# Attention on one core: four pairs of heads turned by transfers, one more group of exponentials on VectorE, and a new order

## The chip, the core and the metric

The kernel runs on one core of one Trainium2 chip. The core's engines work side by side: TensorE (PE) multiplies matrices, VectorE (DVE), ScalarE (ACT) and GpSimd (POOL) work elementwise, and SyncE (SP) issues transfers (DMAs). The metric is the device time of one execution in microseconds. Before the change it was 114.85 us, the median of three runs (114.81 to 115.61).

## The reference

Softmax attention over 8 batches of 8 heads, 512 positions and 64 dimensions, in and out as 32-bit floats:

```python
scale = 1.0 / np.sqrt(q.shape[-1])
scores = np.einsum('bhqd,bhkd->bhqk', q, k) * scale
scores = scores - scores.max(axis=-1, keepdims=True)
attn = np.exp(scores)
attn = attn / attn.sum(axis=-1, keepdims=True)
return np.einsum('bhqk,bhkd->bhqd', attn, v)
```

The kernel subtracts no maximum. It multiplies by a fixed factor within the exponential, and gives `v` a column of ones, so that the sum of the weights comes out of the same matmul as the values; the division stands at the end.

## The kernel before, in words

**Pairs.** The 64 heads are taken as 32 pairs, numbered 0 to 31. For each pair `k`, `q` and `v` are loaded as 256 KB transfers (L487), all issued by SyncE. GpSimd casts them to 16 bits (`cast`): `k` and `q` into a tile `qkp` (L503), `v` into one of twelve tiles `vp` (L493). Seven raw tiles per tensor exist, so a load waits for the cast of the pair seven before it.

**Turning.** The scores need `q` and `k` with the head dimension on the partitions. TensorE transposes eight blocks of 128x128 of `qkp` into a tile of PSUM (`transposes`, L534), and VectorE copies it to `tqk` (`copy`, L547). Pair 0 has its own start (`first_pair`).

**Scores and exponentials.** A group is two blocks of 128 keys by 512 queries. `scores` (L574) writes one group into one of three PSUM tiles `st`. There are 129 groups, the last two of which are the two query halves of one. ScalarE takes the exponential of a group in one instruction (L578) and writes `pt`. Sixteen groups, listed in `ON_DVE`, go to VectorE instead: `raise_` (L598) turns scores into the bits of a 16-bit float, and five passes (L615, L624, L632, L634, L638) correct it. The result is two tiles, `pe` and `pd`, the sum of whose products is wanted, so each such block costs two value matmuls instead of one.

**Values.** `values` (L670) accumulates, for each head, four units of 128 queries by 64 columns and the column of sums. Seven units fill a PSUM tile `o`. VectorE takes the reciprocals (`reciprocal`, L644), multiplies (`normalise`, L649), and writes the units into a ring of 112 units in SBUF. `store` (L660) sends a head (four units, 128 KB) from the ring to memory. All but one of the 63 heads that pass through the ring are stored by SyncE; one, the first head of the last pair, goes out on ScalarE's queue. The very last head has its own path: `last_values` (L686) and `finish` (L699 to L706), which normalises it into `obl` and stores it by SyncE.

**What sets the order.** The class `Plan` plays all engines through with fixed costs in nanoseconds and writes down the order of steps. The kernel is emitted in this order, and on each engine the instructions run in the order in which they are emitted. The plan decides, for each engine, what comes next: SyncE has loads first (`step_sp`), stores when no load is possible or more than `URGENT` stores are outstanding; TensorE has scores first, then transposes, then values (`step_pe`); VectorE has copies, raises, reciprocals and products first, passes in between (`step_dve`). The constants `LATE_...`, `HURRY`, `SOON`, `PAIR`, `DUEK`, `DUEV`, `DUEL` and `PRE` shift these decisions and the times by which casts are due. A transfer that SyncE issues waits in its place for what it needs, and all later ones wait behind it. Eight completion semaphores are used in turn, so that a transfer also waits for the landing of the eighth before it.

In the profile, a line beginning with L is a line of the code below. SPq and ACTq mark issues of transfers by SyncE and by ScalarE.

Of the kernel before, what the change touches and what calls it, by code (L numbers as in the profile page):

```python
# [9 lines left out]
FP32 = mybir.dt.float32  # L10
# [7 lines left out]
class Plan:  # L18
# [15 lines left out]
    STEP = 5  # L34
    CALM, KEEN = 9000, 4
    FIRST_UNIT = 4
    ON_DVE = (5, 11, 15, 24, 36, 41, 49, 55, 60, 70, 76, 83, 94, 105, 109, 120)

    LATE_NORM, LATE_COPY, HURRY, SOON, BACKLOG = 2300, 700, 1000, 200, 700
    LATE_MUL, WAIT = 400, 200  # L40
    SLACK, AHEAD = 0, 2

    CAST, CAST_PORT, CAST_DONE, TO_POOL = 557, 475, 130, 150
    SCALE_PORT, PRODUCT_PORT, GAP, REACH = 265, 533, 20, 5
    FIRST_LAND, LOAD, STORE, LATENCY, ISSUE = 5200, 740, 370, 2300, 470
    QUEUED, URGENT = 3500, 16
    RAW, QK16, NV, NU = 7, 5, 12, 112
    PAIR, DUEK, DUEV, DUEL, PRE = 3300, 2800, 4000, 7000, 0

    def __init__(self, groups, pairs, first):  # L50
        self.groups, self.pairs = groups, pairs
        self.pe, self.act, self.dve = 7000, self.FIRST_EXP, 6300
        self.pool, self.port, self.dma = 4600, 4600, self.FIRST_LAND
        self.m, self.tiled = first, True
        self.read = []
        self.exps = {}
        for m in range(first):
            self.act += self.EXP + self.EXP_FIXED
            self.exps[m] = self.act + self.EXP_DONE
            self.read.append(self.exps[m])  # L60
        self.tq = {0: 5800}
        self.transposed = {0: 5800}
        self.next_t = 1
        self.part_t = 0
        self.banks = [5100, 5800]
        self.todo = [(g, h) for g in range(pairs) for h in range(2)]
        self.last = self.todo.pop()
        self.last_part = 0
        self.head = None
        self.units = self.FIRST_UNIT  # L70
        self.member = {b: m for m, grp in enumerate(groups) for b in grp}
        self.ready = []
        self.passes = []
        self.passed = {}
        self.raised = set()
        self.steps = []
        self.busy_dve = 0
        self.done_heads = 0

        late = {grp[0][0] for m, grp in enumerate(groups) if m in self.ON_DVE}  # L80
        due = []
        for g in range(pairs):
            scores = 5000 + self.PAIR * g
            if g:
                due += [(scores - self.DUEK, g, "k"), (scores - self.DUEK + 10, g, "q")]
            due.append((scores + self.DUEV + (self.DUEL if g in late else 0), g, "v"))
        self.due = sorted(due)
        self.uncast = list(self.due)
        self.casts = []
        self.landed, self.cast_done = {}, {}  # L90
        self.first_loads = [(g, n) for _, g, n in self.due if g < self.RAW]
        self.first_loads += [(self.RAW, "k"), (self.RAW, "q")]
        for x in self.first_loads:
            self.dma += self.LOAD
            self.landed[x] = self.dma
        self.loads, self.stores, self.stored = [], [], []
        self.sp = 1650 + 470 * len(self.first_loads)

    def note(self, t, *what):
# [51 lines left out]
                self.cast_done[(g, n)] = begin + self.CAST + self.CAST_DONE  # L151

    def step_sp(self, t):
        if self.sp > t or self.dma > t + self.QUEUED:
            return
        urgent = len(self.stores) > self.URGENT
        if self.loads and not urgent:
            g, n = self.loads[0]
            if self.cast_done.get((g - self.RAW, n), 1e9) <= t:
                self.loads.pop(0)  # L160
                self.note(t, "load", g, n)
                self.dma = max(self.dma, t + self.LATENCY - self.LOAD) + self.LOAD
                self.landed[(g, n)] = self.dma
                self.sp = t + self.ISSUE
                return
        if self.stores and self.stores[0] <= t:
            self.stores.pop(0)
            self.note(t, "store")
            self.dma = max(self.dma, t + self.LATENCY - self.STORE) + self.STORE
            self.stored.append(self.dma)  # L170
            self.sp = t + self.ISSUE
# [66 lines left out]
    def last_values(self, t):  # L238
        end = len(self.groups)
        if self.m < end or self.last_part == 4:  # L240
            return False
        part = self.last_part
        read = self.exps.get(end - (3, 3, 2, 1)[part], 1e9)
        if t < max(read, self.cast_done.get((self.last[0], "v"), 1e9)):
            return False
        self.note(t, "last", part)
        self.full(t, self.V_UNIT)
        if part == 3:
            self.ready.append((self.pe + self.TO_DVE, "finish", ()))
        self.last_part += 1  # L250
        return True

# [36 lines left out]
    def step_pe(self, t):  # L289
        if self.m == len(self.groups):  # L290
            self.values(t)
            return
        g = self.groups[self.m][0][0]
        backlog = self.act - t
        one, two = self.free() <= t, self.free(1) <= t
        if one and (two or backlog < self.HURRY or self.tiled):
            return self.scores(t)
        if not one and backlog < self.BACKLOG and self.free() < t + self.SOON:
            return
        if self.part_t:  # L300
            return self.transposes(t)
        if (
            self.next_t < self.pairs
            and self.next_t <= g + self.AHEAD
            and all(self.cast_done.get((self.next_t, n), 1e9) <= t for n in "kq")
            and self.bank(t) is not None
        ):
            return self.transposes(t)
        if not self.values(t) and one:
            self.scores(t)  # L310

    def step_dve(self, t):
# [14 lines left out]
        if now:  # L327
# [22 lines left out]
                for _ in range((what[0] + what[1]) // 4 - what[0] // 4):  # L350
                    self.stores.append(self.dve + 100)
            elif kind == "finish":
                self.dve = t + self.RECIPROCAL + self.PASS_DONE + self.NORM[0] + 4 * self.NORM_COLUMN
            elif kind == "copy":
                held, done = self.COPY if what[0] != 1 else self.COPY_1
                self.dve = t + held
                self.banks[what[1]] = self.tq[what[0]] = t + done + self.TO_PE
            else:
                self.dve = t + self.RAISE[0]
                self.read[what[0]] = t + self.RAISE[1] + self.TO_PE  # L360
                self.raised.add(what[0])
                self.passes += [(what[0], s) for s in range(len(self.PASSES))]
                self.passed[what[0], None] = self.dve + self.PASS_DONE
# [43 lines left out]
def kernel(  # L407
# [28 lines left out]
    cpool = ctx.enter_context(tc.tile_pool(name="const", bufs=1))  # L436
    lpool = ctx.enter_context(tc.tile_pool(name="load", bufs=7))
    qpool = ctx.enter_context(tc.tile_pool(name="qk16", bufs=5))
    tpool = ctx.enter_context(tc.tile_pool(name="tqk", bufs=4))
    ppool = ctx.enter_context(tc.tile_pool(name="pt", bufs=24))  # L440
    dpool = ctx.enter_context(tc.tile_pool(name="pd", bufs=4))
    wpool = ctx.enter_context(tc.tile_pool(name="work", bufs=Plan.BITS))
# [83 lines left out]
    def transposes(g, n, bank):  # L526
# [7 lines left out]
            reads[g] = nc.tensor.transpose(tps[g][:, n, i, :], qkp[g][:, n, i, :], ident)  # L534
        if g == 1 and n == 1:
            copy(g, n)

    def copy(g, n=0):
        if g == 1:
# [116 lines left out]

    def store():
        g, h, u0 = heads.pop(0)
        queue = nc.scalar if (g, h) == (LAST, 0) else nc.sync
        queue.dma_start(out=source(out, g)[:, h], in_=ring[:, u0 % NU : u0 % NU + NI, :])  # L660

    def values(g, h, y, u, bank):
# [13 lines left out]
            )  # L676

    def last_values(part):
        if part == 0:
            last["o"] = ps_st.tile([P, 2, S], FP32, tag="st", name="o_last")[  # L680
                :, 0, 0 : NI * (D + 1)
            ].rearrange("p (x d) -> p x d", x=NI)
        half, late = ((0, 0), (1, 0), (0, 1), (1, 1))[part]
        for c in (2 * late, 2 * late + 1):
            for x in (2 * half, 2 * half + 1):
                nc.tensor.matmul(  # L686
                    last["o"][:, x, :],
                    blocks[(LAST, c, 1)][0][:, x * P : (x + 1) * P],
                    vps[LAST % NV][:, 1, c, :],
                    start=(c == 0 and x == 0),  # L690
                    stop=(c == NI - 1),
                    skip_group_check=True,
                )

    def finish():
        o = last["o"]
        ob = opool.tile([P, NI, D], FP32, tag="obl", name="obl", bufs=1)
        rc = opool.tile([P, 7, 1], FP32, tag="rc", name="rc_last")
        nc.vector.reciprocal(out=rc[:, 0:NI], in_=o[:, :, D : D + 1])  # L699
        nc.vector.tensor_tensor(  # L700
            out=ob[:, :, :],
            in0=o[:, :, 0:D],
            in1=rc[:, 0:NI].broadcast_to([P, NI, D]),
            op=AluOp.mult,
        )
        nc.sync.dma_start(out=source(out, LAST)[:, 1], in_=ob[:, :, :])  # L706

    def first_loads():
        tk = load_tile(0, "k")
# [99 lines left out]
    with tc.manual_schedule():  # L809
# [6 lines left out]
        for n in range(NV):  # L816
# [5 lines left out]
            "values": values,  # L822
            "load": load,
            "store": store,
            "cast": cast_behind,
            "raise": raise_,
            "copy": lambda g, b: copy(g),
# [38 lines left out]
```

## Time and profile before

| What | Number |
|---|---|
| median of three runs | 114.85 us |
| the profiled execution | 114.75 us |
| its span, first to last instruction | 113.0 us |
| ScalarE busy | 105.6 us (93%) |
| TensorE busy | 103.8 us (92%) |
| VectorE busy | 101.4 us (90%) |
| GpSimd busy | 64.9 us (57%) |
| bytes moved by transfers | 33.84 MB, 300 GB/s on the mean |

The span is the time from the first instruction to the last; the execution's own time has some more around it. A busy time is the time in which an engine has an instruction running; SyncE has no such number, as issuing isn't counted as busy. Rows of groups give the line, engine and operation, the tiles (out<-in) and their shapes, the count, then busy time and mean length in ns, and the idle time before. Rows of a timeline give start and length in us.

### The profile page before, as it was taken

What the parts mean: (1) busy time and instruction counts of PE and PEld (TensorE: products, weight loads), DVE (VectorE), ACT (ScalarE), POOL (GpSimd) and SP (SyncE); (2) the same over time, 40 slices, a digit from 0 to 9 for tenths busy, and PEclk for the clock granted to TensorE, in tenths of its full rate; (3) what the DMA queues carried; (4) which work ended last, traced back from release to release, by engine and by line L of the source; (5) the groups of instructions that cost most, each with busy time, mean ns of one, the idle gap of its engine ahead of it and who ended that gap; (6) DMA issues with size and microseconds to landing.
All of it is one profiled execution on the core that took longest, in us unless ns stands there. A gap on an engine that the chain in (4) does not pass through costs nothing.

```text
span 113.0 us, 4341 instructions
## 1 busy us (share of the span) xinstructions
PE 103.8 (92%) x1687; PEld 68.9 (61%) x1687; DVE 101.4 (90%) x226; ACT 105.6 (93%) x118; POOL 64.9 (57%) x127
## 2 busy tenths in 40 slices
PE   7979989899999998899999999999999999999940
PEld 2634646567665575575677567677668665775730
DVE  1567999999989999999999999999999999999560
ACT  4699999999999999999999999999999999999930
POOL 2167896275478858668667987846866993000000
PEclk9999999999999999999999999999999999999995
DMA  3999999999999999999999989999993978828744
GB/s 98 273 335 354 349 348 347 346 348 348 348 349 343 345 332 350 348 358 312 340 358 331 292 244 338 339 345 331 369 363 102 298 264 267 275 93 266 249 131 156
DMA packets 35381, 33.84 MB, mean 300 GB/s; under 512 B 2592, under 2 KB 35360, under 8 KB 35360
## 3 DMA queue, kind: packets, MB, share of 16 engines
q1 hardware_dynamic: 34928, 33.17, 91.5%
q10 hardware_dynamic: 432, 0.39, 1.0%
q8 instruction: 13, 0.21, 0.9%
q14 instruction: 8, 0.07, 0.2%
HBM read 25.17 MB, written 8.39 MB: 297 GB/s over the span
## 4 chain that ended last, share of the span: by engine, by line
PE 45%; DVE 42%; ACT 7%; issue 2%
PE o L670 19%; PE st L574 15%; DVE pd L598 9%; DVE tqk L547 8%; DVE ring L649 7%; PE tp L534 7%; ACT pt L578 7%; DVE m L632 4%; DVE pd L638 3%; PE st_0a L717 3%; DVE pe L624 2%; DVE m L615 2%; DVE m L634 2%; DVE rc L644 2%; PE st L760 1%
## 5 line engine op out<-in xcount | busy, mean ns | idle before, releaser
L578 ACT ACTIVATE pt<-st 128x1024 f16<-128x1024 f32 (+1 forms) x110 | 100.4, 1096 | 0.0
L670 PEld LDWEIGHTS <-pt 128*128 128x128 f16 x880 | 38.9, 98 | 12.6 <-issue 10.8
L670 PE MATMUL o<-vp,pt 128*128 128x65 f16 x880 | 46.3, 194 | 0.2
L574 PE MATMUL st<-tqk 64*128 64x512 f16 (+1 forms) x250 | 42.4, 381 | 2.5 <-ACT pt L578 1.8
L503 POOL CAST qkp<-k 128x512 f16<-128x512 f32 x31 | 21.5, 693 | 11.6 <-DMA k<-in_k_dram 5.2
L493 POOL CAST vp<-v 128x512 f16<-128x512 f32 x32 | 21.7, 696 | 7.9 <-DVE rc L644 2.6
L503 POOL CAST qkp<-q 128x512 f16<-128x512 f32 x30 | 21.3, 710 | 6.7 <-DVE rc L644 3.3
L649 DVE TENSOR_TENSOR ring<-o,rc 128x448 f32<-128x448 f32 (+2 forms) x37 | 22.4, 607 | 0.6
L670 PE MATMUL o<-vp,pe 128*128 128x65 f16 x128 | 22.1, 195 | 0.0
L670 PE MATMUL o<-vp,pd 128*128 128x65 f16 x128 | 21.9, 193 | 0.0
L534 PE MATMUL tp<-ident,qkp 128*128 128x128 f16 x248 | 19.9, 220 | 1.0 <-DVE ring L649 0.7
L547 DVE COPY tqk<-tp 128x1024 f16<-128x1024 f16 x30 | 20.4, 680 | 0.2 <-PE tp L534 0.2
L598 DVE TENSOR_SCALAR pd<-st 128x1024 uint16<-128x1024 f32 x16 | 19.5, 1218 | 0.7 <-PE st L574 0.7
L534 PEld LDWEIGHTS <-qkp 128*128 128x128 f16 x248 | 14.3, 97 | 7.9 <-issue 4.0
L574 PEld LDWEIGHTS <-tqk 64*128 64x128 f16 x250 | 11.6, 93 | 11.7 <-issue 4.3
L670 PEld LDWEIGHTS <-pe 128*128 128x128 f16 x128 | 12.5, 98 | 3.8 <-issue 2.9
L670 PEld LDWEIGHTS <-pd 128*128 128x128 f16 x128 | 12.6, 98 | 0.0
L638 DVE TENSOR_TENSOR pd<-pd,m 128x1024 f16<-128x1024 f16 x16 | 10.9, 683 | 0.0
L632 DVE TENSOR_TENSOR m<-m 128x1024 f16<-128x1024 f16 x16 | 10.9, 683 | 0.0
L644 DVE RECIPROCAL rc<-o 128x7 f32<-128x7 f32 (+2 forms) x37 | 7.3, 198 | 1.9 <-PE o L670 1.9
L624 DVE TENSOR_SCALAR pe<-pd 128x1024 uint16<-128x1024 uint16 x16 | 6.8, 424 | 0.0
L615 DVE TENSOR_SCALAR m<-pd 128x1024 uint16<-128x1024 uint16 x16 | 6.6, 413 | 0.0
(50 smaller groups left out, 33.3 us busy)
## 6 DMA issues: line engine op xcount, KB each, us to landing
v<-in_v_dram SPq DMA_DIRECT2D x32, 256.0 KB, 5.8
k<-in_k_dram SPq DMA_DIRECT2D x31, 256.0 KB, 5.9
q<-in_q_dram SPq DMA_DIRECT2D x31, 256.0 KB, 5.8
out_dram<-ring SPq DMA_DIRECT2D x62, 128.0 KB, 3.7
k<-in_k_dram ACTq DMA_DIRECT2D x2, 128.0 KB, 2.8
q<-in_q_dram SPq DMA_DIRECT2D x2, 128.0 KB, 2.6
out_dram<-ring ACTq DMA_DIRECT2D x1, 128.0 KB, 1.9
out_dram<-obl SPq DMA_DIRECT2D x1, 128.0 KB, 2.0
```

Source lines behind the costliest of these rows:

```text
L493: return nc.gpsimd.tensor_copy(out=vps[g % NV][:, :, :, 0:D], in_=raw[g]["v"][:, :, :, :])
L503: return nc.gpsimd.tensor_copy(out=dst, in_=src[:, :, :, :])
L534: reads[g] = nc.tensor.transpose(tps[g][:, n, i, :], qkp[g][:, n, i, :], ident)
L547: nc.vector.tensor_copy(out=tqk[g][:, :, :], in_=tps.pop(g).rearrange("p n i c -> p n (i c)"))
L574: nc.tensor.matmul(st[:, x, cols], kc, qc[:, cols], start=True, stop=True)
L578: nc.scalar.activation(out=pt[:, :, cols], in_=st[:, :, cols], func=EXP, scale=scale, bias=SHIFT)
L598: nc.vector.tensor_scalar(out=r["pd"][:, :, :], in0=r["st"][:, :, :], scalar1=BITS, scalar2=BIAS, op0=AluOp.mult, op1=AluOp.add,)
L632: ins = nc.vector.tensor_tensor(out=m16, in0=m16, in1=m16, op=AluOp.mult)
L638: ins = nc.vector.tensor_tensor(out=u16, in0=u16, in1=m16, op=AluOp.mult)
L644: dve(nc.vector.reciprocal(out=rcs[u][:, 0:n], in_=o[:, x : x + n, D : D + 1]))
L649: nc.vector.tensor_tensor(out=ring[:, u % NU : u % NU + n, :], in0=o[:, x : x + n, 0:D], in1=rcs.pop(u)[:, 0:n].broadcast_to([P, n, D]), o ...
L670: nc.tensor.matmul(os[u // 7][:, u % 7, :], part[:, y * P : (y + 1) * P], vps[g % NV][:, h, c, :], start=(n == 0), stop=(n == len(parts) - 1),
```

## The change

The planner gets a new step, `turn`. Pairs 28 to 31 (`TURNED = 28`) are no longer transposed by TensorE and copied by VectorE. SyncE issues one transposing transfer for each, from `qkp` straight into `tqk`, of which there are now eight tiles instead of four. The casts of `k` and `q` of these pairs are made due earlier (`TURN_AHEAD`). `ON_DVE` lists 17 groups instead of 16, at other places. The last head is handled in two halves of the queries: two tiles for its values, two reciprocals and products, two stores of 64 KB by SyncE. The last two stores from the ring go out on ScalarE's queue. Other constants of the plan are changed, so that the whole order is made anew: the places of casts, loads, stores and passes differ all through the kernel.

On SyncE, the changed kernel issues 163 transfers in place of 159. Ahead of the first `turn` stand 123: all loads but one, and stores. Then follow: the turn of pair 28 (issue 124), the load of the last `v`, nine stores, the turns of pairs 29 and 30 (135 and 136), eight stores, the turn of pair 31 (145), sixteen stores, and the two halves of the last head (162 and 163).

```diff
--- before.py
+++ after.py
@@ -34,18 +34,20 @@
     STEP = 5
     CALM, KEEN = 9000, 4
     FIRST_UNIT = 4
-    ON_DVE = (5, 11, 15, 24, 36, 41, 49, 55, 60, 70, 76, 83, 94, 105, 109, 120)
-
-    LATE_NORM, LATE_COPY, HURRY, SOON, BACKLOG = 2300, 700, 1000, 200, 700
-    LATE_MUL, WAIT = 400, 200
+    ON_DVE = (5, 11, 17, 24, 30, 39, 45, 54, 59, 69, 75, 79, 88, 96, 104, 112, 120)
+
+    LATE_NORM, LATE_COPY, HURRY, SOON, BACKLOG = 1100, 1800, 700, 160, 700
+    LATE_MUL, WAIT = 1200, 200
     SLACK, AHEAD = 0, 2
 
     CAST, CAST_PORT, CAST_DONE, TO_POOL = 557, 475, 130, 150
-    SCALE_PORT, PRODUCT_PORT, GAP, REACH = 265, 533, 20, 5
+    SCALE_PORT, PRODUCT_PORT, GAP, REACH = 271, 537, 20, 5
     FIRST_LAND, LOAD, STORE, LATENCY, ISSUE = 5200, 740, 370, 2300, 470
     QUEUED, URGENT = 3500, 16
     RAW, QK16, NV, NU = 7, 5, 12, 112
-    PAIR, DUEK, DUEV, DUEL, PRE = 3300, 2800, 4000, 7000, 0
+    TURNED, TQ = 28, 8
+    TURN, TURN_LATENCY, TURN_ISSUE, TURN_AHEAD, TURN_MARGIN = 2500, 4300, 1450, 7500, 200
+    PAIR, DUEK, DUEV, DUEL, PRE = 3300, 3550, 5500, 1000, 1250
 
     def __init__(self, groups, pairs, first):
         self.groups, self.pairs = groups, pairs
@@ -82,7 +84,8 @@
         for g in range(pairs):
             scores = 5000 + self.PAIR * g
             if g:
-                due += [(scores - self.DUEK, g, "k"), (scores - self.DUEK + 10, g, "q")]
+                ahead = self.DUEK if g < self.TURNED else self.TURN_AHEAD
+                due += [(scores - ahead, g, "k"), (scores - ahead + 10, g, "q")]
             due.append((scores + self.DUEV + (self.DUEL if g in late else 0), g, "v"))
         self.due = sorted(due)
         self.uncast = list(self.due)
@@ -94,6 +97,7 @@
             self.dma += self.LOAD
             self.landed[x] = self.dma
         self.loads, self.stores, self.stored = [], [], []
+        self.turn = self.TURNED
         self.sp = 1650 + 470 * len(self.first_loads)
 
     def note(self, t, *what):
@@ -151,7 +155,19 @@
                 self.cast_done[(g, n)] = begin + self.CAST + self.CAST_DONE
 
     def step_sp(self, t):
-        if self.sp > t or self.dma > t + self.QUEUED:
+        if self.sp > t or (self.loads and self.dma > t + self.QUEUED):
+            return
+        g = self.turn
+        if (
+            g < self.pairs
+            and self.m > self.member[(g - self.TQ, 3, 1)]
+            and max(self.cast_done.get((g, n), 1e9) for n in "kq") + self.TURN_MARGIN <= t
+        ):
+            self.note(t, "turn", g)
+            self.dma = max(self.dma, t + self.TURN_LATENCY - self.TURN) + self.TURN
+            self.tq[g] = self.transposed[g] = self.dma
+            self.sp = t + self.TURN_ISSUE
+            self.turn += 1
             return
         urgent = len(self.stores) > self.URGENT
         if self.loads and not urgent:
@@ -240,13 +256,13 @@
         if self.m < end or self.last_part == 4:
             return False
         part = self.last_part
-        read = self.exps.get(end - (3, 3, 2, 1)[part], 1e9)
+        read = self.exps.get(end - (3, 2, 2, 1)[part], 1e9)
         if t < max(read, self.cast_done.get((self.last[0], "v"), 1e9)):
             return False
         self.note(t, "last", part)
         self.full(t, self.V_UNIT)
-        if part == 3:
-            self.ready.append((self.pe + self.TO_DVE, "finish", ()))
+        if part % 2:
+            self.ready.append((self.pe + self.TO_DVE, "finish", (part // 2,)))
         self.last_part += 1
         return True
 
@@ -300,7 +316,7 @@
         if self.part_t:
             return self.transposes(t)
         if (
-            self.next_t < self.pairs
+            self.next_t < self.TURNED
             and self.next_t <= g + self.AHEAD
             and all(self.cast_done.get((self.next_t, n), 1e9) <= t for n in "kq")
             and self.bank(t) is not None
@@ -350,7 +366,7 @@
                 for _ in range((what[0] + what[1]) // 4 - what[0] // 4):
                     self.stores.append(self.dve + 100)
             elif kind == "finish":
-                self.dve = t + self.RECIPROCAL + self.PASS_DONE + self.NORM[0] + 4 * self.NORM_COLUMN
+                self.dve = t + self.RECIPROCAL + self.PASS_DONE + self.NORM[0] + 2 * self.NORM_COLUMN
             elif kind == "copy":
                 held, done = self.COPY if what[0] != 1 else self.COPY_1
                 self.dve = t + held
@@ -436,7 +452,7 @@
     cpool = ctx.enter_context(tc.tile_pool(name="const", bufs=1))
     lpool = ctx.enter_context(tc.tile_pool(name="load", bufs=7))
     qpool = ctx.enter_context(tc.tile_pool(name="qk16", bufs=5))
-    tpool = ctx.enter_context(tc.tile_pool(name="tqk", bufs=4))
+    tpool = ctx.enter_context(tc.tile_pool(name="tqk", bufs=Plan.TQ))
     ppool = ctx.enter_context(tc.tile_pool(name="pt", bufs=24))
     dpool = ctx.enter_context(tc.tile_pool(name="pd", bufs=4))
     wpool = ctx.enter_context(tc.tile_pool(name="work", bufs=Plan.BITS))
@@ -534,6 +550,13 @@
             reads[g] = nc.tensor.transpose(tps[g][:, n, i, :], qkp[g][:, n, i, :], ident)
         if g == 1 and n == 1:
             copy(g, n)
+
+    def turn(g):
+        tqk[g] = tpool.tile([P, 2, S], FP16, tag="tqk", name=f"tqk_{g}")
+        nc.sync.dma_start_transpose(
+            out=tqk[g].rearrange("p n (i c) -> p (n i) c", c=P),
+            in_=qkp[g].rearrange("p n i c -> p (n i c)"),
+        )
 
     def copy(g, n=0):
         if g == 1:
@@ -656,7 +679,8 @@
 
     def store():
         g, h, u0 = heads.pop(0)
-        queue = nc.scalar if (g, h) == (LAST, 0) else nc.sync
+        left = 2 * NP - 1 - (u0 + NI - Plan.FIRST_UNIT) // NI
+        queue = nc.scalar if left < 2 else nc.sync
         queue.dma_start(out=source(out, g)[:, h], in_=ring[:, u0 % NU : u0 % NU + NI, :])
 
     def values(g, h, y, u, bank):
@@ -676,34 +700,36 @@
             )
 
     def last_values(part):
-        if part == 0:
-            last["o"] = ps_st.tile([P, 2, S], FP32, tag="st", name="o_last")[
-                :, 0, 0 : NI * (D + 1)
-            ].rearrange("p (x d) -> p x d", x=NI)
-        half, late = ((0, 0), (1, 0), (0, 1), (1, 1))[part]
+        half, late = part // 2, part % 2
+        if not late:
+            last[half] = ps_st.tile([P, 2, S], FP32, tag="st", name=f"o_last{half}")[
+                :, 0, 0 : 2 * (D + 1)
+            ].rearrange("p (x d) -> p x d", x=2)
         for c in (2 * late, 2 * late + 1):
-            for x in (2 * half, 2 * half + 1):
+            for x in range(2):
                 nc.tensor.matmul(
-                    last["o"][:, x, :],
-                    blocks[(LAST, c, 1)][0][:, x * P : (x + 1) * P],
+                    last[half][:, x, :],
+                    blocks[(LAST, c, 1)][0][:, (2 * half + x) * P : (2 * half + x + 1) * P],
                     vps[LAST % NV][:, 1, c, :],
                     start=(c == 0 and x == 0),
                     stop=(c == NI - 1),
                     skip_group_check=True,
                 )
 
-    def finish():
-        o = last["o"]
-        ob = opool.tile([P, NI, D], FP32, tag="obl", name="obl", bufs=1)
-        rc = opool.tile([P, 7, 1], FP32, tag="rc", name="rc_last")
-        nc.vector.reciprocal(out=rc[:, 0:NI], in_=o[:, :, D : D + 1])
+    def finish(half):
+        o = last[half]
+        ob = opool.tile([P, 2, D], FP32, tag="obl", name=f"obl{half}", bufs=2)
+        rc = opool.tile([P, 7, 1], FP32, tag="rc", name=f"rc_last{half}")
+        nc.vector.reciprocal(out=rc[:, 0:2], in_=o[:, :, D : D + 1])
         nc.vector.tensor_tensor(
             out=ob[:, :, :],
             in0=o[:, :, 0:D],
-            in1=rc[:, 0:NI].broadcast_to([P, NI, D]),
+            in1=rc[:, 0:2].broadcast_to([P, 2, D]),
             op=AluOp.mult,
         )
-        nc.sync.dma_start(out=source(out, LAST)[:, 1], in_=ob[:, :, :])
+        nc.sync.dma_start(
+            out=source(out, LAST)[:, 1, 2 * half : 2 * half + 2], in_=ob[:, :, :]
+        )
 
     def first_loads():
         tk = load_tile(0, "k")
@@ -822,6 +848,7 @@
             "values": values,
             "load": load,
             "store": store,
+            "turn": turn,
             "cast": cast_behind,
             "raise": raise_,
             "copy": lambda g, b: copy(g),
```

## The prediction

> **What bounds the kernel now.** I read the page first, then the busy time by stretch, then SyncE's own timeline of transfer issues, which decides the matter.
>
> ```profile
> span 113.0 us, 4341 instructions
> PE 103.8 (92%) x1687; PEld 68.9 (61%) x1687; DVE 101.4 (90%) x226; ACT 105.6 (93%) x118; POOL 64.9 (57%) x127
> ...
> L578 ACT ACTIVATE pt<-st 128x1024 f16<-128x1024 f32 (+1 forms) x110 | 100.4, 1096 | 0.0
> ```
>
> The span is 113.0 us, the execution 114.75 us, so 1.75 us lie around the span. The sum is made against 114.75; the median, 114.85, is 0.1 above it, and I add that at the end. ScalarE has no idle time in its exponentials (the 0.0 at the end of its row). VectorE and TensorE are close behind:
>
> ```profile
> core 0: us, PE busy (x) PEld busy (x) DVE busy (x) ACT busy (x) POOL busy (x), PEclk, DMA share, GB/s
> 10.00:100.00 90.00, 86.83 (x1466) 58.71 (x1465) 88.82 (x184) 90.00 (x99) 60.88 (x115) 1.00 1.00 321
> ...
> 88.00:106.00 18.00, 17.87 (x306) 11.63 (x305) 17.31 (x37) 18.00 (x20) 6.03 (x11) 1.00 0.75 244
> ```
>
> In 10 to 100 us ScalarE is busy for all of 90.0 us and VectorE for 88.8. So three engines are full. A fourth one is full as well and appears in no busy column: SyncE, which issues transfers one at a time, in a written order. Its timeline near the end (start, length to the end of the last of the group, count):
>
> ```profile
> 86.33 1.93 SPq L660 DMA_DIRECT2D out_dram<-ring  x4
> 88.35 0.39 SPq L487 DMA_DIRECT2D v<-in_v_dram  x1
> 88.79 20.58 SPq L660 DMA_DIRECT2D out_dram<-ring  x32
> 109.54 0.38 SPq L706 DMA_DIRECT2D out_dram<-obl  x1
> 109.97 0.44 SPq L660 DMA_DIRECT2D out_dram<-ring  x1
> ```
>
> These are the last of SyncE's 159 issues (2+31+31+32 loads, 62+1 stores). From the end, the ring store at 109.97 is issue 159, `obl` is 158, the group of 32 is 126 to 157, the load at 88.35 is 125, and the last of the group of four is 124. Are those 32 stores waiting for data, or are they late? Count what VectorE still has to write:
>
> ```profile
> L649 DVE TENSOR_TENSOR ring<-o,rc x10: 425/622/625, 88.5 to 108.5; 128x448 f32<-128x448 f32 x9, 128x256 f32<-128x256 f32 x1
> L660 SPq DMA_DIRECT2D out_dram<-ring x30: 383/415/2287, 87.9 to 105.7; - x30
> ```
>
> A head is four units of 64 columns. From 88.5 on, VectorE writes 9x7+4 = 67 units, under 17 heads. At 88.79, 33 stores on SyncE and one on ScalarE's queue are outstanding: 34 heads. So some 17 finished heads stand in line. The 30 stores of the second row are issued from 87.9 to 105.7, with one load among them: 17.9/30 = 0.60 us apiece, though an issue itself takes 0.415 us. The single places that the change will touch:
>
> ```profile
> 94.52 0.44 SPq L660 DMA_DIRECT2D out_dram<-ring  x1
> 101.36 0.41 SPq L660 DMA_DIRECT2D out_dram<-ring  x1
> 105.75 0.44 SPq L660 DMA_DIRECT2D out_dram<-ring  x1
> 106.69 2.69 SPq L660 DMA_DIRECT2D out_dram<-ring  x3
> ```
>
> The stores that start at 94.52, 101.36 and 105.75 are issues 135, 145 and 154. Between the last two, the pitch is 4.39/9 = 0.49 us. The rest of the 0.60 is long issues, such as the one of 2.29 us beside which the transfer view of 98 to 101 us shows a 16 KB block of instructions coming in:
>
> ```profile
> q8 instruction: 1, 0.02, 3.8%
> ```
>
> Only at 106.19 (105.75+0.44) does SyncE run out of work, and it waits until 106.69. **That 0.5 us is all the slack that SyncE has from issue 124 to the end**, and the end is its last store: issued by 110.41, 2.6 us before the span ends.
>
> **The change, part by part.** The 17th group on VectorE takes one exponential from ScalarE: 100.4/110 = 0.91 us less. VectorE gets one raise and five passes, and loses four copies:
>
> ```profile
> L547 DVE COPY tqk<-tp 128x1024 f16<-128x1024 f16 x30 | 20.4, 680 | 0.2 <-PE tp L534 0.2
> L598 DVE TENSOR_SCALAR pd<-st 128x1024 uint16<-128x1024 f32 x16 | 19.5, 1218 | 0.7 <-PE st L574 0.7
> L638 DVE TENSOR_TENSOR pd<-pd,m 128x1024 f16<-128x1024 f16 x16 | 10.9, 683 | 0.0
> L632 DVE TENSOR_TENSOR m<-m 128x1024 f16<-128x1024 f16 x16 | 10.9, 683 | 0.0
> L624 DVE TENSOR_SCALAR pe<-pd 128x1024 uint16<-128x1024 uint16 x16 | 6.8, 424 | 0.0
> L615 DVE TENSOR_SCALAR m<-pd 128x1024 uint16<-128x1024 uint16 x16 | 6.6, 413 | 0.0
> L634 DVE TENSOR_SCALAR m<-m 128x1024 f16<-128x1024 f16 x16 | 6.6, 411 | 0.0
> ```
>
> That is 1.218+0.683+0.683+0.424+0.413+0.411 = 3.83 us more and 4x0.68 = 2.72 us less: +1.1 us, against 90.0-88.8 = 1.2 us of idle time in 10 to 100 us. It just fits, so the 0.91 us can be had, and no more. TensorE loses 32 transposes and gains eight value matmuls:
>
> ```profile
> 95.83 0.61 PE tp L534 x8
> ...
> 98.67 1.22 PE o L670 x32
> ```
>
> 4x0.61 = 2.4 us off, 8x1.22/32 = 0.3 us on; neither is the limit once ScalarE is, so I count nothing. The last head in halves and the last ring store moved to ScalarE's queue spare the issue that now stands behind `obl` (109.97 against 109.54): 0.43 us, if SyncE is free at that time. ScalarE has ended its exponentials by then, so its two issues cost nothing.
>
> What has a price is the four transposing transfers, all issued by SyncE. In the changed order they are issues 124, 135, 136 and 145 of 163; the last 16 ring stores follow as 146 to 161, and the two halves of `obl` as 162 and 163. What stands ahead of issue 124 is the same as before in number and bytes (all loads but one, the same stores), so I let SyncE arrive there at the same time. From there on the queue has 163-159 = 4 more issues: the ring store given to ScalarE is made good by the second half of `obl`. **Every store to the end stands behind them, in one queue with 0.5 us of slack.** A transposing transfer of issue time I adds I plus the 0.07 us between issues (0.49-0.42), so the end moves by 4x(I+0.07)-0.5.
>
> No transposing transfer is in this trace, so I must be bounded. Below: it issues like any transfer, 0.42 us whatever its size. Above: its destination is eight blocks of 128x128, and each costs an issue of its own, 8x0.42 = 3.4 us. Neither row is nearer: it is one instruction, as below, over eight blocks, as above. I take the middle of the two by ratio, the root of 0.42x3.4, 1.2 us. Below nothing it can't go, since it is added to the queue. The sum: 4x1.27-0.5 = 4.6 us. Last issue 110.41+4.6 = 115.0, span 117.6, time 117.6+1.75 = 119.3, with the median's 0.1 **119.4 us**.
>
> The Trainium skill has two rules here, at odds. Its page "Advanced Engine Details and Errata", section "X-Bar Transpose (TRN2)", says that transposing transfers are as fast as plain ones; for the issue that would be the lower end, 116.2 us, which is a rival below. Its page "DMA: Bandwidth & Descriptors" gives 262,144 sequencer cycles for 8,192 tiles on earlier generations, 32 a tile, and a tile of 16x128; with 64 tiles and the 1.2 GHz of "Clock Domains" an estimate is 1.7 us, and the sum would be 121.4 us. No run here shows either so far.
>
> The second wait is TensorE's, for the turned pair. Scores now start, for pairs 29 and 31 (the tiles are pair 29's four, pair 30's four and pair 31's five, counted back from the last), at
>
> ```profile
> 96.37 0.39 PE L574 MATMUL st<-tqk 64*128 64x512 f16 x2
> ...
> 103.56 1.03 PE L574 MATMUL st<-tqk 64*128 64x512 f16 x4
> ...
> DMA to landing us min/median/max: 3.3/4.0/4.6
> ...
> DMA to landing us min/median/max: 1.8/1.8/4.1
> ...
> v<-in_v_dram SPq DMA_DIRECT2D x32, 256.0 KB, 5.8
> ```
>
> The first landing row is that of the two 256 KB loads issued in 84 to 90 us, the nearest in size and place: 3.3 us for the one with least ahead of it. Pair 29's transfer starts at 94.52 plus what 124 costs over a store, 0.8, so 95.3; it lands 3.3+0.8 later, at 99.4: 3.0 us late. Meanwhile values, and all else behind the first scores of pair 29 on TensorE, stand still, and ScalarE runs dry once its three score tiles are read. Pair 31's starts at 101.36+3x0.8 = 103.8, lands at 107.9, against 103.56+3.0 = 106.6: 1.3 us more. So arithmetic ends 4.3-0.9 = 3.4 us later than now:
>
> ```profile
> 109.09 0.42 DVE L700 TENSOR_TENSOR obl<-o_last,rc_last 128x256 f32<-128x256 f32 x1
> ```
>
> that is 109.5+3.4 = 112.9, still ahead of the time at which SyncE reaches the last half of `obl`, 109.97+4.6 = 114.6. The stall is hidden behind the queue as long as it stays under 114.6-109.5+0.9 = 6.0 us. The landing's bounds are 1.8 us (the second row, ring stores of 88 to 106 us at best) and 5.8 us (the third, loads of the whole kernel). At 1.8 the stall is smaller and still hidden. At 5.8 it is 5.5+1.3 = 6.8 us, 0.8 past the cover, and the time 120.2 us.
>
> The rest of the new order (earlier casts, other places of the groups, eight `tqk` tiles for four) changes no duration, and I count it at nothing: POOL, which casts, is busy 60.9 of the 90 us, and what of a cast comes later falls into its idle third. If that cover is gone, the price shows up as scores waiting for a cast.
>
> **The rivals.**
>
> *The issue is cheap* (I = 0.42), as that of 256 KB loads is:
>
> ```profile
> L487 SPq DMA_DIRECT2D v<-in_v_dram x10: 368/419/1927, 61.8 to 88.4; - x10
> ```
>
>  The end moves by 4x0.49-0.5 = 1.5 us: 116.3 us with the median's 0.1. For: a plain issue does not depend on size, 0.42 us for 256 KB as for 128. Against: eight blocks in one instruction. Chance 0.17.
>
> *SyncE comes to issue 124 early: faster.* The whole price hangs on its lateness there. Between its first store and issue 124 it isn't always issuing:
>
> ```profile
> 45.83 1.04 SPq L660 DMA_DIRECT2D out_dram<-ring  x2
> ```
>
> From 45.83 (issue 62) to 87.88 (issue 124) it spends 42.0 us on 62 issues, 0.68 apiece, 11.8 us over the 0.49 pitch, on landings of earlier transfers, casts and long issues. If the new order wins back 4.6 of them, the queue no longer ends last, and pair 29's transfer starts at 90.7, in time. Then the gains remain: 114.85-0.91-0.43 = 113.5 us. That is the point from which it decides: issue 124 under way by about 83.5 us. Against: the same bytes go through transfers that are busy without a break for most of that stretch (share 1.00 in 10 to 100 us), and the blocks of instructions come at the same counts. Chance 0.11.
>
> *The issue is as dear as eight* (I = 3.4). 4x3.47-0.5 = 13.4 us: 128 us. Chance 0.07.
>
> *The queue gains a little, or the issue is very short*, and it ends within 1% of before: beyond the parts above, chance 0.07.
>
> **How the numbers follow.** The forecast, I between 0.8 and 2.0 us, has 0.58 and runs from 117.7 to 122.6. Slower by over 1% (what a measurement of this kernel can tell) are the forecast, most of the cheap issue and the dear one: 0.81; within 1% 0.08; faster 0.11. The range of 115.0 to 122.5 holds the forecast, the cheap issue and the last rival, and leaves out the faster end (0.11) and the dear one (0.07).
>
> **What would show it.** In the changed kernel SyncE's transposing issues start near 88, 95, 97 and 104 us and take about 1.2 us each; its stores then run without a wait up to the two `obl` issues, which start after VectorE has ended, near 114. TensorE's scores of pair 29 wait some 3 us for a transfer into `tqk`, and ScalarE, now without idle time, shows a gap of 2 to 3 us near 97 to 100. The groups read 17 raises and 26 copies. It is wrong if issue 124 comes before 84 us, if a transposing issue takes 0.4 us, or if ScalarE shows no gap and `obl` is issued as soon as it is written.

## The result and the profile after

The changed kernel takes 119.5 us (median of four runs, 118.59 to 122.48) where the kernel before takes 114.9: it is slower, 1.0365 times the time before, 95% interval 1.0325 to 1.0405. The run of 122.48 us, which had the lowest granted clock of the four (0.963), is left out of this ratio, as runs like it are left out of the ratios below. The profiled execution took 119.54 us, its span 117.8. The page of the changed kernel, its first line and two of its groups (out<-in, count, busy us, mean ns, then idle us before them and what ended most of it):

```profile
span 117.8 us, 4317 instructions
...
L601 ACT ACTIVATE pt<-st 128x1024 f16<-128x1024 f32 (+1 forms) x109 | 99.9, 1106 | 4.2 <-PE st L597 4.1
...
L597 PE MATMUL st<-tqk 64*128 64x512 f16 (+1 forms) x250 | 42.4, 384 | 5.0 <-DMA tqk<-qkp 3.4
```

Of the kernel before, the row of TensorE's scores:

```profile
L574 PE MATMUL st<-tqk 64*128 64x512 f16 (+1 forms) x250 | 42.4, 381 | 2.5 <-ACT pt L578 1.8
```

ScalarE, which had no idle time in its exponentials, now has 4.2 us, and of the 5.0 us that TensorE's scores wait, 3.4 are for turned tiles; before, they waited 2.5 us, most of it for ScalarE. That looks like the whole loss. It isn't; SyncE's timeline (start, length to the end of the last of the group, count) shows what sets the end:

```profile
87.96 1.33 SPq L556 DMA_TRANSPOSE tqk<-qkp  x1
89.39 0.52 SPq L503 DMA_DIRECT2D v<-in_v_dram  x1
90.01 5.50 SPq L684 DMA_DIRECT2D out_dram<-ring  x9
95.61 2.63 SPq L556 DMA_TRANSPOSE tqk<-qkp  x2
98.34 5.79 SPq L684 DMA_DIRECT2D out_dram<-ring  x8
104.23 1.24 SPq L556 DMA_TRANSPOSE tqk<-qkp  x1
105.52 9.14 SPq L684 DMA_DIRECT2D out_dram<-ring  x16
114.75 0.89 SPq L730 DMA_DIRECT2D out_dram<-obl  x2
```

The four turns start at 88.0, 95.6, 97.0 and 104.2 us; sixteen ring stores follow the last; only then come the two halves of the last head, at 114.75. VectorE's last product, by its own timeline, had been ready for two microseconds:

```profile
112.54 0.29 DVE L724 TENSOR_TENSOR obl<-o_last,rc_last 128x128 f32<-128x128 f32 x1
```

So arithmetic ends at 112.83 us and SyncE's last issue at 115.64. Before, these were 109.51 and 110.41. The turns' own rows, from the view of their line (ns of an issue and us to landing, each as least, median, most):

```profile
L556 SPq DMA_TRANSPOSE tqk<-qkp x4: 1237/1266/1331, 88.0 to 104.2; - x4
...
DMA to landing us min/median/max: 3.1/3.3/3.4
```

### The profile page after: what moved, and what is told of

The parts are those of the page before. It is cut to its first block, busy times and chain, and to the rows that moved or that the text cites. A ratio compares the mean times of both kernels' runs of the same rounds, so it can differ in the third digit from the quotient of the medians.

```text
span 117.8 us, 4317 instructions
## 1 busy us (share of the span) xinstructions
PE 103.4 (88%) x1663; PEld 67.6 (57%) x1663; DVE 101.5 (86%) x230; ACT 105.1 (89%) x117; POOL 66.0 (56%) x127
## 4 chain that ended last, share of the span: by engine, by line
DVE 54%; PE 15%; ACT 11%; DMA 9%; issue 4%; POOL 2%; SPq 0%; ACTq 0%; POOLq 0%
ACT pt L601 11%; DVE pd L621 11%; DVE tqk L570 9%; DVE ring L672 9%; PE st L597 6%; DVE pd L661 6%; DVE m L655 6%; DMA tqk<-qkp 6%; PE o L694 5%; DVE m L657 3%; DVE m L638 3%; DVE pe L647 3%; DMA q<-in_q_dram 2%; DVE rc L667 2%; PE tp L550 2%
## 5 line engine op out<-in xcount | busy, mean ns | idle before, releaser
L694 PEld LDWEIGHTS <-pt 128*128 128x128 f16 x872 | 40.3, 99 | 14.4 <-issue 13.2
L694 PE MATMUL o<-vp,pe 128*128 128x65 f16 x136 | 23.2, 195 | 0.0
L694 PE MATMUL o<-vp,pd 128*128 128x65 f16 x136 | 23.0, 193 | 0.0
L621 DVE TENSOR_SCALAR pd<-st 128x1024 uint16<-128x1024 f32 x17 | 20.7, 1218 | 1.6 <-PE st L597 1.6
L550 PE MATMUL tp<-ident,qkp 128*128 128x128 f16 x216 | 17.1, 220 | 0.8 <-DVE ring L672 0.6
L570 DVE COPY tqk<-tp 128x1024 f16<-128x1024 f16 x26 | 17.7, 679 | 0.1
L550 PEld LDWEIGHTS <-qkp 128*128 128x128 f16 x216 | 12.5, 97 | 7.9 <-issue 4.2
L694 PEld LDWEIGHTS <-pe 128*128 128x128 f16 x136 | 13.3, 98 | 3.2 <-issue 2.7
L661 DVE TENSOR_TENSOR pd<-pd,m 128x1024 f16<-128x1024 f16 x17 | 11.9, 699 | 0.0
L657 DVE TENSOR_SCALAR m<-m 128x1024 f16<-128x1024 f16 x17 | 7.2, 425 | 0.1
```

What stands on the lines that cost most here:

```text
L570: nc.vector.tensor_copy(out=tqk[g][:, :, :], in_=tps.pop(g).rearrange("p n i c -> p n (i c)"))
L621: nc.vector.tensor_scalar(out=r["pd"][:, :, :], in0=r["st"][:, :, :], scalar1=BITS, scalar2=BIAS, op0=AluOp.mult, op1=AluOp.add,)
L657: ins = nc.vector.tensor_scalar(out=m16, in0=m16, scalar1=CUBIC, scalar2=LINEAR, op0=AluOp.mult, op1=AluOp.add)
L661: ins = nc.vector.tensor_tensor(out=u16, in0=u16, in1=m16, op=AluOp.mult)
L694: nc.tensor.matmul(os[u // 7][:, u % 7, :], part[:, y * P : (y + 1) * P], vps[g % NV][:, h, c, :], start=(n == 0), stop=(n == len(parts) - 1),
```

## The experiments

Two theories were on the table. By the **queue theory**, the end is SyncE's last issue: the turns are issues of about 1.3 us in a queue that has no slack, whether or not anyone waits for what they turn. By the **stall theory**, the end moves because TensorE and ScalarE wait for the turned tiles. The first four runs separate the two.

**Four plain transfers more (q_plain).** In the kernel before, with spare tiles of SBUF:

```diff
+    def extra():
+        issued[0] += 1
+        for _ in range({124: 1, 134: 2, 142: 1}.get(issued[0], 0)):
+            dst = spare[issued[1]]
+            issued[1] += 1
+            nc.sync.dma_start(out=dst.rearrange("p n c -> p (n c)"), in_=scratch[:, :])
```

`extra` is called ahead of each issue of SyncE in `load` and `store`.

> The kernel before, with four more plain transfers of 256 KB on SyncE's queue, from one spare tile of SBUF into others that nothing reads, as issues 124, 135, 136 and 145 (where the changed kernel has its turns). Nobody waits for them. Queue theory (SyncE's queue has 0.5 us of slack after issue 124, and its last issue sets the end): 4 x 0.49 - 0.5 = 1.5 us longer, 116.3 us. Stall theory (the changed kernel is slower because TensorE waits for the turned tiles): no wait, so no change, 114.9 us.

Measured: 116.5 us, ratio 1.0167 (1.0091 to 1.0243), that is 1.9 us (1.0 to 2.8) longer. The view of the added line, and the end of SyncE's timeline:

```profile
L490 SPq DMA_DIRECT2D spare<-scratch x4: 471/502/599, 87.7 to 100.8; - x4
...
DMA to landing us min/median/max: 2.3/2.3/2.7
...
110.74 0.44 SPq L720 DMA_DIRECT2D out_dram<-obl  x1
111.24 0.44 SPq L674 DMA_DIRECT2D out_dram<-ring  x1
```

These issues took 0.50 us (median), not 0.42; with that the formula gives 4x0.57-0.5 = 1.8 us. The stall theory's "no change" lies outside the interval.

**Four turns that nobody reads (q_turn).**

```diff
-            nc.sync.dma_start(out=dst.rearrange("p n c -> p (n c)"), in_=scratch[:, :])
+            nc.sync.dma_start_transpose(out=dst[:, :, :], in_=scratch[:, :])
```

> The same, with transposing transfers of 256 KB in the place of the plain ones, again into tiles that nothing reads. With the 1.27 us that a turn's issue took in the changed kernel, the queue theory has 4 x (1.27 + 0.07) - 0.5 = 4.9 us longer, 119.7 us, without any wait of TensorE or gap on ScalarE. Stall theory: 114.9 us, since nothing is turned that anyone needs.

Measured: 119.16 us, ratio 1.0354 (1.0286 to 1.0423), 4.1 us (3.3 to 4.9) longer. The added line, the end of SyncE's timeline, VectorE's last product and ScalarE's exponentials from 92 us on:

```profile
L490 SPq DMA_TRANSPOSE spare<-scratch x4: 1237/1274/1377, 86.9 to 102.4; - x4
...
DMA to landing us min/median/max: 2.8/3.1/3.6
...
112.85 0.39 SPq L720 DMA_DIRECT2D out_dram<-obl  x1
113.30 0.44 SPq L674 DMA_DIRECT2D out_dram<-ring  x1
...
109.00 0.42 DVE L714 TENSOR_TENSOR obl<-o_last,rc_last 128x256 f32<-128x256 f32 x1
...
91.48 16.66 ACT L590 ACTIVATE pt<-st 128x1024 f16<-128x1024 f32 x19
```

Arithmetic ends at 109.42 us, as before, and ScalarE has no gap (its row is one block of 19). Yet the last head is stored 3.4 us after it was ready. Four issues that touch nothing the kernel needs make nearly the whole loss. The 4.9 us expected lie at the upper edge of the interval. In the profiled execution, the shortest of the four (117.84 us), SyncE's last issue ends 3.3 us later than in the kernel before, and the first of the four turns starts at 86.86, a microsecond before issue 124 of that kernel.

**The change without its stall (no_stall).**

```diff
-                kc = tqk[g][s, 1, c * P : (c + 1) * P]
-                qc = tqk[g][s, 0, :]
+                t = tqk[min(g, Plan.TURNED - 1)]
+                kc = t[s, 1, c * P : (c + 1) * P]
+                qc = t[s, 0, :]
```

> The changed kernel, whose turns are issued as before, but the scores of pairs 28 to 31 read the turned tile of pair 27 instead of their own (so these pairs' scores are not those of the reference), and no score waits for a turn. Queue theory: the wait of 3.4 us on TensorE and ScalarE's gap of 4.2 us go, SyncE's last issue stays near 115.6 us, and the time stays at 119.5 us (at most 0.5 off). Stall theory: the time falls by the 3.4 to 4.2 us, to 115.3 to 116.1 us.

Measured: ratio 1.0381 (1.0289 to 1.0474), 119.3 us by that, not to be told from the changed kernel's 1.0365. SyncE's first turn, ScalarE's and VectorE's rows, and SyncE's last:

```profile
89.01 1.33 SPq L556 DMA_TRANSPOSE tqk<-qkp  x1
...
91.59 16.01 ACT L602 ACTIVATE pt<-st 128x1024 f16<-128x1024 f32 x18
...
108.23 0.29 DVE L725 TENSOR_TENSOR obl<-o_last,rc_last 128x128 f32<-128x128 f32 x1
...
115.19 0.90 SPq L731 DMA_DIRECT2D out_dram<-obl  x2
```

The stall is gone, arithmetic ends at 108.5 us, 1.0 earlier than in the kernel before, and nothing of it is seen in the time: the last head waits 6.7 us for its issue. SyncE came to its issue 124 a microsecond later in this trace than in that of the changed kernel (89.01 against 87.96), and ended its last at 116.09 in place of 115.64; that shift is too small to hide the 3.4 to 4.2 us that the stall theory asks for. The stall theory falls.

**The change with fewer issues (paired).** Where the two heads of a pair lie side by side in the ring, the first call of `store` keeps back, and the second issues both (`joined` is worked out from the plan's order of heads):

```diff
+        if (g, h, u0) in joined:
+            held.append((g, h, u0))
+            return
+        if held:
+            u0 = held.pop()[2]
+            queue.dma_start(
+                out=source(out, g),
+                in_=ring[:, u0 % NU : u0 % NU + 2 * NI, :].rearrange("p (h i) d -> p h i d", h=2),
+            )
+            return
```

> The changed kernel with the stores of a pair's two heads joined into one transfer of 256 KB wherever they lie side by side in the ring (24 issues fewer on SyncE; the same bytes, the last pairs' stores stay single). Queue theory: 24 x 0.49 = 11.8 us of issuing go, pair 29's turn comes before 92 us and pair 31's before 99, the last two issues wait for VectorE, and what the change saves elsewhere shows: 113.5 us, under the kernel before. If the turning transfers hurt in another way (by their bytes or by what they do to other transfers), it stays above 115 us.

Measured: **112.88 us**, ratio 0.983 (0.9789 to 0.987): 2.0 us under the kernel before, faster than both. (23 pairs of stores were joined, one fewer than expected.) The turns of pairs 29 and 31, SyncE's last issues, and VectorE's last product:

```profile
88.66 3.69 SPq L556 DMA_TRANSPOSE tqk<-qkp  x2
...
96.31 1.24 SPq L556 DMA_TRANSPOSE tqk<-qkp  x1
...
108.29 0.84 SPq L742 DMA_DIRECT2D out_dram<-obl  x2
...
108.37 0.29 DVE L736 TENSOR_TENSOR obl<-o_last,rc_last 128x128 f32<-128x128 f32 x1
```

The same four turns, in the same planned order, are now in time (88.7 in place of 95.6 us, 96.3 in place of 104.2), and the last head is issued as soon as VectorE has written it. The bytes are the same; what changed is the number of issues.

The time is 0.6 us below the 113.5 expected. The span is 1.8 us shorter than before, in three parts: arithmetic ends 0.85 us earlier (108.66), SyncE's last issue ends 0.47 us behind it in place of 0.90, and the span ends 2.07 us behind that issue in place of 2.6. The third part was not forecast, and its cause stays open: in tail_only below, where the last transfer of SyncE is the same half head, it is 2.57 us.

**Is joining worth it by itself? (before_paired)** The same edit of `store` in the kernel before.

> The kernel before, with the stores of a pair's two heads joined wherever they lie side by side (as in paired), and nothing else of the change. Queue theory: in the kernel before SyncE catches up 0.5 us before the end anyway and VectorE's last product at 109.5 us sets the end, so joining gives 0 to 0.5 us: 114.4 to 114.9 us, and the gain of paired (2.0 us) comes from the change once its queue is free. If joining is worth 2 us by itself, 112.9 us, and the change added nothing.

Measured: 114.9 us, ratio 0.9983 (0.9947 to 1.0018): no difference. (25 pairs of stores were joined.) So the 2.0 us of the run before come from the change, once its queue is free. Whether SyncE was ahead of the work here, as expected, is not shown.

**The change without its turns (no_turn).**

```diff
-    TURNED, TQ = 28, 8
+    TURNED, TQ = 32, 8
```

> The changed kernel without the turns: the boundary is set to 32, so TensorE transposes and VectorE copies all pairs, and the planner orders the 17 groups, the halved last head and the stores anew. By the prediction's sum VectorE gains 3.83 us of work against 1.2 us of idle time: 2.6 us longer, less 0.4 at the tail, 117.0 us; SyncE's queue, with 159 issues, isn't last. If the 17th group could be had without the turns, 113.5 us.

Measured: 116.89 us, ratio 1.0166 (1.0122 to 1.0209). Its last product, and its busy time from 10 to 100 us by engine (columns as in the prediction's table):

```profile
111.72 0.41 DVE L672 TENSOR_TENSOR ring<-o,rc 128x256 f32<-128x256 f32 x1
...
10.00:100.00 90.00, 85.33 (x1402) 56.31 (x1399) 89.69 (x185) 89.78 (x99) 62.04 (x116) 1.00 1.00 319
```

VectorE is busy for 89.7 of 90 us, and ends at 112.1 us instead of 109.5. In this plan a 17th group doesn't fit beside the copies of all pairs: the turns are what makes room for it. Whether other constants of the plan could fit it was not tried.

**The tail alone (tail_only).** In the kernel before, only `last_values`, `finish` and the queue of the last two ring stores are those of the changed kernel, with the plan's steps for them.

> The kernel before with the halved last head and two last ring stores on ScalarE's queue, and nothing else of the change; SyncE's queue is one ring store shorter and one half head longer. The prediction has 0.43 us less, 114.4 us. If SyncE is late for its last issues anyway, no change, 114.9 us.

Measured: ratio 0.9994 (0.9961 to 1.0027), from 0.45 us less to 0.3 more. Neither value is excluded with any force, but the trace says why so little came:

```profile
109.07 1.06 SPq L707 DMA_DIRECT2D out_dram<-obl  x2
...
109.48 0.29 DVE L701 TENSOR_TENSOR obl<-o_last,rc_last 128x128 f32<-128x128 f32 x1
```

Two more instructions on VectorE end its work at 109.77 in place of 109.51, so the last issue ends at 110.13 instead of 110.41: 0.28 us in this execution, not 0.43.

**The turns earlier in the queue (told).**

```diff
-    FIRST_LAND, LOAD, STORE, LATENCY, ISSUE = 5200, 740, 370, 2300, 470
+    FIRST_LAND, LOAD, STORE, LATENCY, ISSUE = 5200, 740, 370, 2300, 650
```

> The changed kernel with one constant of the planner changed: an issue of SyncE is planned at 650 ns in place of 470, near the 0.60 us that the stores really took. The planner then puts the turns ahead of more stores (issues 118, 127, 128 and 134 in place of 124, 135, 136 and 145) and nine ring stores behind the last head's. The turns come in time, near 83, 89, 91 and 95 us, and no score waits. Queue theory: the same 163 issues still have to go through one queue, its last one near 115 to 116.5 us, so the time stays at 119 to 120 us. Stall theory: 114 to 115 us.

Measured: ratio 1.0276 (1.0207 to 1.0345), 118.1 us by that. The turns and the end of SyncE's timeline:

```profile
81.99 1.34 SPq L556 DMA_TRANSPOSE tqk<-qkp  x1
...
88.10 3.36 SPq L556 DMA_TRANSPOSE tqk<-qkp  x2
...
95.01 1.24 SPq L556 DMA_TRANSPOSE tqk<-qkp  x1
...
108.42 0.83 SPq L730 DMA_DIRECT2D out_dram<-obl  x2
109.31 4.35 SPq L684 DMA_DIRECT2D out_dram<-ring  x9
```

No score waits, the last head goes out as soon as it is written, and nine finished heads are still in line behind it, the last issued by 113.66. The turns' place in the queue cures the stall and not the time. The time is a microsecond under what was expected: SyncE came to its issue 118 at 81.99, where the changed kernel began its own at 83.64.

```profile
83.64 0.48 SPq L684 DMA_DIRECT2D out_dram<-ring  x1
```

Why this order gets there earlier wasn't looked into.

## Why the prediction was right, point by point

- **SyncE comes to issue 124 at the same time as before.** 87.96 us against 87.88. This carried everything else, and the rival that denied it fell with it. That it is true to a tenth is luck: with the same 123 issues ahead, the other traces have 86.86 (q_turn), 87.70 (q_plain) and 89.01 us (no_stall).
- **The issue time of a turn**, chosen between 0.42 and 3.4 us as the middle by ratio, 1.2: measured 1.24 to 1.33 (in told and in paired one turn each took longer, 1.89 and 2.29 us). The size came out well from a wide bracket; that was luck as much as method. The rival with 0.42 us fell, and the one with 3.4.
- **4x(I+0.07)-0.5.** With the measured mean, 1.28, it gives 4.9 us; SyncE's last issue ends 115.64-110.41 = 5.2 us later, and the span grew by 4.8, since it ends 117.8-115.64 = 2.2 us behind that issue, against 2.6 before. Why these differ is not shown.
- **The wait of TensorE.** Forecast 3.0 us for pair 29, measured 3.06, though three terms were off and cancelled, which is luck: the transfer started 0.3 us later than forecast, it landed 3.3 us after its start with the long issue already in it, where the prediction had added 0.8 for that, and TensorE came to these scores 0.4 us earlier (99.04-3.06 = 95.98, in place of 96.37). For pair 31 the forecast was 1.3 us, and 0.3 was measured. The row in TensorE's timeline of the changed kernel, with the idle time and what ended it, and the sum over the kernel:

```profile
99.04 0.39 PE L597 MATMUL st<-tqk 64*128 64x512 f16 x2 [3.06 <-DMA tqk<-qkp]
...
PE st L597 <- DMA tqk<-qkp: 3.4, 2, 3.1
```

- **The stall is hidden behind the queue.** Arithmetic was to end at 112.9 us and did at 112.83, still 2 us ahead of the issue of the last half; without the stall the time didn't move (no_stall). That 112.9 was hit so closely is luck as well: the stall of pair 31 was 1.0 us too long in the forecast, and ScalarE's gap of 1.2 us that the last section describes was not in it.
- **The gain of 0.91 us from the 17th group** is there once the queue is free: arithmetic ends 1.0 us earlier in no_stall and 0.85 in paired. Both have the rest of the new order too, so the group's own share is argued from the size. That it just fits VectorE is shown by paired and, from the other side, by no_turn (2.0 us longer, 2.2 forecast).
- **The tail's 0.43 us** is a term that was mis-sized: 0.28 us in the trace of tail_only, and none that the runs could tell. The prediction left out the two instructions that halving adds to VectorE's end. The 0.43 between the end of arithmetic and that of SyncE's last issue is there in paired. In the changed kernel it was without weight.
- **The two rules of the Trainium skill.** That transposing transfers are as fast as plain ones ("Advanced Engine Details and Errata", "X-Bar Transpose (TRN2)") does not hold for the issue, 1.27 us against 0.42. It does hold behind the issue: landing is counted from the start of the issue, and the turns of q_turn landed after 3.1 us (median), the plain transfers of q_plain, of the same size from the same tile, after 2.3; the 0.8 us between them is what the issue takes longer (1.27 against 0.50). The 32 sequencer cycles a tile, worked out from the table against "previous generations" in "DMA: Bandwidth & Descriptors" (section "Why a DMA increments its semaphore by 16 and not by 1"), from which an estimate of 1.7 us was made, are nearer but high: with the same 1.2 GHz, 1.27 us is 24 cycles for each of 64 tiles. An issue time by tiles fits; no run here varied the number of tiles.
- **Small slips of the sums.** 116.2 and 117.7 us lack the median's 0.1 (116.3 and 117.8), the 11.8 us over the pitch are 42.05-62x0.49 = 11.7, and 87.88-4.6 is 83.3, not 83.5. Nothing rests on them.

## What to carry to other kernels

An engine that issues transfers is a pipeline stage like any other, and no busy column shows it: compare the finished work not yet issued with the work still to come, and the time of an issue with the pitch at which issues leave. Moving work from a full compute engine to "the DMAs" was paid in issues here, and with finished stores in line each issue moved the end, whoever read the result. Before reordering such a queue, try to shorten it: joining 23 pairs of stores turned a loss of 4.6 us into a gain of 2.0, where joining 25 in the kernel before gained nothing; setting the turns earlier in the queue (told) left a loss of 3.2.

## What the runs showed that was not expected

TensorE falls to half its clock soon after its wait. Of the changed kernel, from 96 to 104 us (busy us and count by engine, then the granted clock, the transfers' share and GB/s):

```profile
core 0: us, PE busy (x) PEld busy (x) DVE busy (x) ACT busy (x) POOL busy (x), PEclk, DMA share, GB/s
...
96.00:98.00 2.00, 0.00 (x0) 0.00 (x0) 1.65 (x5) 1.15 (x2) 0.75 (x2) 1.00 0.89 194
98.00:100.00 2.00, 0.96 (x17) 0.73 (x18) 0.00 (x0) 0.47 (x1) 0.00 (x0) 0.91 1.01 216
100.00:102.00 2.00, 2.00 (x25) 1.07 (x23) 0.88 (x3) 0.83 (x2) 0.61 (x1) 0.50 0.86 273
102.00:104.00 2.00, 2.00 (x37) 1.48 (x36) 1.11 (x3) 2.00 (x3) 0.09 (x1) 0.74 0.17 54
```

After 3.06 us without a matmul TensorE starts again at 99.04. If the clock is either full or half, the 0.91 of 98 to 100 us puts its fall near 99.6 and the 0.74 of 102 to 104 its return near 103.0. In between ScalarE, fed by TensorE, gets another gap, the second below (idle us and what ended it in brackets):

```profile
99.53 1.02 ACT L601 ACTIVATE pt<-st 128x1024 f16<-128x1024 f32 x1 [2.38 <-PE st L597]
101.72 2.85 ACT L601 ACTIVATE pt<-st 128x1024 f16<-128x1024 f32 x3 [1.17 <-PE st L597]
```

In no_stall, without the wait, the granted clock stays at 1.00 in the same stretches, and ScalarE has no such gap (two stretches of it, columns as above):

```profile
100.00:102.00 2.00, 2.00 (x42) 1.24 (x39) 2.00 (x5) 1.96 (x4) 0.00 (x0) 1.00 0.68 190
102.00:104.00 2.00, 2.00 (x38) 1.31 (x35) 2.00 (x6) 2.00 (x3) 0.00 (x0) 1.00 0.64 206
```

So the wait brings both, the half clock and the second gap; that the gap comes from the clock is read from the order of events, and no run separates them. The Trainium skill's page "TensorE: Matmul & The Clock Gate" ("Part 1: The HAM clock gate") gives half the clock as the state after at least one idle window of some 3.4 us, a window that runs freely. The 0.50 agrees with that; the length does not quite, since here a gap of 3.06 us, shorter than the window, was enough. These 1.2 us stand where the prediction had a longer stall of pair 31. They were hidden by the queue as well.

A plain issue of SyncE for 256 KB took 0.50 us from SBUF to SBUF (q_plain, median) against 0.42 us for a load from memory. The two transfers differ in the shape of their rows too, and no run separates that from the place.
